# A hybrid decoder trunk: transposes moved out of gate and up, and 64-byte offsets for the last moving weights and the cross queries

## The chip, the cores and the metric

The kernel runs on one core of a Trainium2 chip. The metric is the device time of one execution in microseconds (us). Times of before are the median of three timed runs; one more execution was recorded by the hardware profiler, and every row shown comes from it.

## The reference

Two layers of a decoder trunk work on x of 256 tokens x 1024 features, in float32. Each layer adds four blocks to x, each on an RMS-normalised copy:

```python
for l in range(DEPTH):                       # DEPTH = 2, SEQ = 256, D_MODEL = 1024, D_FF = 2816
    x = x + 0.5 * swiglu(rms_norm(x, ffn1_norm[l]), ffn1_w_gate[l], ffn1_w_up[l], ffn1_w_down[l])
    x = x + hybrid_mixer(rms_norm(x, mix_norm[l]), w_in[l], ...)       # HGRN2 heads | FoX heads
    x = x + memory_cross_attention(rms_norm(x, cross_norm[l]), rms_norm(mem, mem_norm[l]), ...)
    x = x + 0.5 * swiglu(rms_norm(x, ffn2_norm[l]), ffn2_w_gate[l], ffn2_w_up[l], ffn2_w_down[l])
return rms_norm(x, final_norm)

def swiglu(h, w_gate, w_up, w_down):
    return (jax.nn.silu(h @ w_gate) * (h @ w_up)) @ w_down
```

The cross attention has 4 heads of 256 features against 256 memory tokens. All weights together are some 217 MB, read once.

## The kernel before

**Products.** Each float32 operand is split into a high part, its cast to fp32r, and a low part, the rest. A product is then three matmuls that add up in PSUM: high by high, high by low, low by high. `mm3` (L448) issues them from lines 449, 450 and 451. In the names of a matmul, `out<-a,b` lists the moving operand `a` first and the stationary one `b` second: the array holds `b` (128 x 128), a LDWEIGHTS loads it, and `a` streams through with 256 or 512 columns. TensorE loads the next `b` while it streams the present `a`.

**Two forms of a projection.** `xstat` and `xstat_first` keep the features `xf` stationary and stream 512 weight columns (`acc<-whi,xfh`, 128x512); the result has tokens on the partitions. `wstat` (L573) keeps weights stationary and streams the 256 tokens (`acc<-xfh,whi`, 128x256); the result has features on the partitions. A feed-forward (`ffn`, L686) takes its 2816 hidden features in six chunks (`FCH`): chunk 0 by `xstat_first`, the other five by `wstat`, gate and then up. Since chunk 0's product `sil` has tokens on the partitions, the task `h_task` (L691) turns it with eight transposes `hp` (L700), and ACT and DVE write its split `hth`, `htl`. In the first feed-forward `first_chunk` does chunk 0 on x itself and turns the factors of the norm with two transposes `rt` (L565). `rows_to_residual` (L644) then does the down projection: for each 128 hidden features, 12 matmuls of 512 columns.

**Weights.** `plan` lists all weight pieces in the order of use. SP issues their loads into three `raw` buffers; ACT casts the high part `whi`, DVE subtracts to get the low part `wlo` (`split`, L177), into seven slots of `wp`. Each entry of `plan` has a `lead`: the place in the slot, in elements of 4 bytes, where the piece begins. It is `LEAD` = 16 (64 bytes) for weights that become stationary and 0 for those that stream. The slots and the buffers of pool `sp` (tag `s4`, which hold `xf`, `hth`, `kc` and `qc` among others) are whole multiples of 256 bytes long and begin at the same place modulo 256. So `lead` alone sets how the address of a weight lies to that of a feature, modulo 256 bytes: 0 or 64.

**Order.** The program is written by `drive` (L410), which runs generators as tasks on an estimated clock; `yield (LAT_HT,)` puts a task's next step that much later, and an `Event` lets it wait for another task. Each engine then does its instructions in the order in which they were written. `lower_bounds` (L312) is one such task: it waits 20 us and 6 us, turns a small table by the transpose `lbt` (L317) and works out the gates' bounds on ACT and DVE. In `cross` (L1115), `head` computes one head's scores `cs` from keys `kc` (moving) and queries `qc` (stationary), and its softmax `pp` is turned and split into `ppT`.

Of the kernel before, what the change touches and what calls it, by code (L numbers as in the profile page):

```python
# [17 lines left out]
P = 128  # L18
# [7 lines left out]
EPS = 1e-6  # L26
NEG = -1.0e30
FCH = [(c, min(512, DFF - c)) for c in range(0, DFF, 512)]

ROWS, LEAD = 1024, 16  # L30
SLOT = ROWS + 128
APART = 64
N_S4, N_W = 19, 7
TAIL = 6
HP = 100
LA_D, LA_S = 3, 1
# [1 line left out]
LAT_LVL, LAT_AX, LAT_HN = 4.0, 1.5, 5.2  # L38
LAT_FS, LAT_FT, LAT_CQ, LAT_CS, LAT_CT = 7.0, 3.5, 2.6, 5.6, 3.0
LAT_Q, LAT_G1, LAT_G2, LAT_M = 5.0, 9.0, 2.0, 18.0  # L40
LAT_HT = 2.4
LAT_FK, LAT_LANE = 6.5, 2.8

OFF_Q, OFF_F, OFF_I, OFF_G = 0, 512, 1024, 1536
# [4 lines left out]
def hymba_kernel(  # L49
# [9 lines left out]
    rawp = ctx.enter_context(tc.tile_pool(name="rawp", bufs=3))  # L59
    wp = ctx.enter_context(tc.tile_pool(name="wp", bufs=N_W))  # L60
    sp = ctx.enter_context(tc.tile_pool(name="sp", bufs=N_S4))
    np_ = ctx.enter_context(tc.tile_pool(name="np", bufs=1))
    sm = ctx.enter_context(tc.tile_pool(name="sm", bufs=4))
    psa = ctx.enter_context(tc.tile_pool(name="psa", bufs=4, space=PSUM))
# [17 lines left out]
    def smp(name="smp"):  # L82
        return pss.tile([P, 512], F32, name=nm(name), tag="smp")

    sp.tile([P, APART], F32, name="apart", tag="apart", bufs=1)
    xs = cp.tile([P, NT, D], F32, name="xs")


# [2 lines left out]
    def kview(w, l, c0, cw, k0, nk):  # L91
        return w[l, k0 * P:(k0 + nk) * P, c0:c0 + cw].rearrange("(k p) c -> p k c", p=P)

    def add_cols(w, l, c0, cw, scaled=None, lead=LEAD):
        for k0 in range(0, KT, 4):
            plan.append((kview(w, l, c0, cw, k0, 4), 4, cw, (scaled[0], scaled[1] + k0) if scaled else None, lead))

    def add_rows(w, l, nkt):
        for k0 in range(0, nkt, 2):
            plan.append((kview(w, l, 0, D, k0, 2), 2, D, None, 0))  # L100

    def add_ffn(g, u, d, l, scaled=None):
        for c0, cw in FCH:
            for w in (g, u):
                add_cols(w, l, c0, cw, scaled, LEAD if c0 else 0)
        add_rows(d, l, FT)

    for l in range(DEPTH):
        add_ffn(ffn1_g, ffn1_u, ffn1_d, l, ("first", 0) if l == 0 else None)
        for o in (OFF_I, OFF_G, OFF_F, OFF_Q):  # L110
            add_cols(w_in, l, o, 512, None, 0 if o in (OFF_I, OFF_G) else LEAD)
        add_cols(w_in, l, OFF_FV + 260, 260, None, 0)
        add_cols(w_in, l, OFF_FQ, 512)
        add_cols(w_in, l, OFF_FK, 512)
        add_cols(w_in, l, OFF_FV, 260, None, 0)
        of_mem = ("mem", 8 * l)
        add_cols(c_wk, l, 0, 512, of_mem)
        add_cols(c_wk, l, 512, 512, of_mem)
        add_cols(c_wv, l, 0, 512, of_mem, 0)
        add_rows(w_out, l, KT)  # L120
        add_cols(c_wv, l, 512, 512, of_mem, 0)
        for c0 in (0, 512):
            add_cols(c_wq, l, c0, 512)
        add_rows(c_wo, l, KT)
        add_ffn(ffn2_g, ffn2_u, ffn2_d, l)

    raws = []
# [73 lines left out]
    def take():  # L201
        i = taken[0]
        taken[0] += 1
        split(i + LA_S)
        return pieces[i]
# [106 lines left out]
    def lower_bounds():  # L312
        nc.sync.dma_start(out=lbr[0:8], in_=hgrn_lb.rearrange("d (h p) -> (d h) p", p=P))
        nc.sync.dma_start(out=lbr[8:24], in_=mem_norm.rearrange("d (k p) -> (d k) p", p=P))
        yield (6.0,)
        pt = smp("lbt")
        nc.tensor.transpose(pt[:, 0:24], lbr, ident[0:24, 0:24])  # L317
# [10 lines left out]
        nc.scalar.activation(e, e, AF.Exp)  # L328
# [74 lines left out]

    clock = [0.0]
    tasks = []

    def spawn(gen):
        tasks.append([gen, clock[0], None])
# [45 lines left out]
        mm3(ps[t][:, :cw], f.hi(kt, t), f.lo(kt, t), pc[0], pc[1], kt == 0, kt == KT - 1)  # L454
        return 3 * 0.107 * max(1.0, cw / 256.0)

    def xstat(f, cw, ps):
        ps += [acc() for _ in range(NT)]
        for kb in range(2):
            pc = take()  # L460
            for j in range(4):
                c = 0.0
                for t in range(NT):
                    c += xmm(ps, f, 4 * kb + j, t, pc[j], cw)
                yield c
# [23 lines left out]
    def first_chunk(f, psa_, psb_):  # L489
# [67 lines left out]
            for t in range(NT):  # L557
                inv_rms(sums[t], rs[t])
        yield 16 * T512
        yield from xstat(f, 512, psb_)  # L560
        rb = sq[0].rearrange("p (j t) -> p j t", j=8)
        pt = smp("rt")
        for t in range(NT):
            nc.vector.tensor_scalar(out=rb[:, t, :], in0=ident, scalar1=0.0, scalar2=rs[t], op0=ALU.mult, op1=ALU.add)
            nc.tensor.transpose(pt[:, t * P:(t + 1) * P], rb[:, t, :], ident)  # L565
        row = sm.tile([P, S], F32, name=nm("L"), tag="L", bufs=1)
        nc.vector.tensor_copy(out=row, in_=pt[:, 0:S])
# [118 lines left out]
    def ffn(cur, nxt_w, last=False, first=False):  # L686
        f = cur.f
        hts = {}
        evs = [Event() for _ in FCH]

        def h_task(c, hs, cw):  # L691
            yield (LAT_HT,)
            nk = cw // P
            hi = s4([P, 4, S], F32R, "hth")
            lo = s4([P, 4, S], F32R, "htl")
            hts[c] = (hi, lo)
            for t in range(NT):
                pt = smp("hp")
                for j in range(nk):
                    nc.tensor.transpose(pt[:, j * P:(j + 1) * P], hs[:, t, j * P:(j + 1) * P], ident)  # L700
# [18 lines left out]
        for ci, (c0, cw) in enumerate(FCH):  # L719
# [7 lines left out]
            else:  # L727
# [20 lines left out]

                yield from wstat(f, use_u, cw)
                evs[ci].fire(3.0)  # L750
        nxt = Next(nxt_w, last)

        def act(kt, t):
            hi, lo = hts[kt // 4]
            return hi[:, kt % 4, t * P:(t + 1) * P], lo[:, kt % 4, t * P:(t + 1) * P]

        yield from rows_to_residual(act, FT, scale, TAIL, nxt, lambda kt: evs[kt // 4])
        return nxt


    def hgrn(q, f, k, v, gw, oT, masks, ready, done):
# [96 lines left out]
            yield 4 * T1  # L858
        done.fire(1.6)


    def pp(rows=P, dt=F32):
        return sm.tile([rows, 512], dt, name=nm("pp"), tag="pp", bufs=4)

    def fox_gates(zb, L_, R_, tri, sel, done):

# [63 lines left out]
    def fox_lane(lane, fq, fk, fv, L_, R_, oT, cmask, oh, ready, done):  # L930
        yield ready
        for pr in (lane, lane + 2):
# [22 lines left out]
            for sub in range(2):  # L955
                pt = smp("fpt")
                for j in range(3):
                    nc.tensor.transpose(pt[:, j * P:(j + 1) * P], prs[sub][:, j * P:(j + 1) * P], ident)
                yield 3 * T1
                pT = sm.tile([P, 512], F32, name=nm("ppT"), tag="ppT", bufs=4)  # L960
# [154 lines left out]
    def cross(cur, kc, vc, mf, nxt_w):  # L1115
# [4 lines left out]
        def head(c, b, qh, ql):  # L1120
# [21 lines left out]
            ph = sm.tile([P, 512], F32R, name=nm("ppT"), tag="ppT", bufs=4)  # L1142
            pl = sm.tile([P, 512], F32R, name=nm("ppT"), tag="ppT", bufs=4)
            put_split(ph, pl, pt)
            yield (LAT_CT,)
            po = smp("cpo")
# [14 lines left out]
        for c in range(2):  # L1161
            oT.alloc(c)

            def use(b, psq):
                q2 = s4([P, 2, 2, S], F32R, "qc")
                put_split(q2[:, 0], q2[:, 1], psq.rearrange("p (k t) -> p k t", k=2))
                spawn(head(c, b, q2[:, 0], q2[:, 1]))

            yield from wstat(f, use)
        nxt = Next(nxt_w)  # L1170
# [8 lines left out]
    def trunk():  # L1179
# [2 lines left out]

        def early():
            yield (20.0,)
            yield from lower_bounds()
            consts.extend(consts_mixer())

        spawn(early())
        for l in range(DEPTH):
# [34 lines left out]
```

## Time and profile before

| what | value |
|---|---|
| median of three timed runs | 1221.28 us (1220.73 to 1222.85) |
| the profiled execution | 1216.61 us, of it 1214.8 us from its first to its last instruction |
| busy: PE, weight loads (PEld), DVE, ACT | 1201.1, 1104.8, 769.8, 651.5 us |
| matmuls of lines 449 to 451 | 2534 of each line |
| read from HBM | 216.23 MB, 179 GB/s over the span |

A matmul's own duration is longer than the step to the next one, since matmuls overlap in the array: with 256 columns it reads about 0.28 us, with 512 about 0.39 us. The step between the starts of two neighbours tells the pace. "Idle before" is time in which an engine had nothing to do ahead of an instruction, and the releaser behind the arrow is what ended it. Because PE is nearly always busy, the rows to look at are those of PE's pace, not of waits.

### The profile page before, as it was taken

The page shows a single profiled execution, that of the slowest core. Times are in us where ns is not written, and L with a number is a line of the kernel's source. Part 1 is how long each engine was busy: PE and PEld are TensorE (multiplying, and loading weights), DVE is VectorE, ACT ScalarE, POOL GpSimd, SP SyncE. Part 2 cuts the span into 40 slices and gives each one's busy share as a digit, 9 for nine tenths or more (in the row PEclk, how much of TensorE's full clock was granted, in tenths as well). Part 3 has the DMA queues.
Part 4 walks back from the last instruction along what each step waited for, and adds up shares of the span by engine and source line. Part 5 has one row for each costly group of instructions (what it writes and reads, how often), then busy time and mean ns, then how long its engine had stood idle before and what let it go on. Part 6 is the DMA issues. An engine that isn't in the chain of part 4 may idle for free.

```text
span 1214.8 us, 21577 instructions
## 1 busy us (share of the span) xinstructions
PE 1201.1 (99%) x9037; PEld 1104.8 (91%) x9037; DVE 769.8 (63%) x1194; ACT 651.5 (54%) x1022; POOL 37.7 (3%) x50
## 2 busy tenths in 40 slices
PE   9999999999999999999999999999999999999997
PEld 7999888999889889998889998889988898999986
DVE  6966647488866675464474565476787766655643
ACT  7665535578854454354264454266686555544532
POOL 0000000011000000000000000000110000000000
PEclk9999999999999999999999999999999999999999
DMA  8655655544544374566474556464444534555740
GB/s 300 209 193 184 246 174 191 176 141 139 197 142 165 106 259 150 198 204 213 139 252 147 208 188 229 139 226 158 144 154 171 193 119 139 183 201 174 245 172 35
DMA packets 100002, 218.68 MB, mean 180 GB/s; under 512 B 4128, under 2 KB 16704, under 8 KB 99904
## 3 DMA queue, kind: packets, MB, share of 16 engines
q1 hardware_dynamic: 99744, 217.03, 52.6%
q8 instruction: 71, 1.16, 0.4%
q10 hardware_dynamic: 160, 0.27, 0.1%
q14 instruction: 27, 0.22, 0.1%
HBM read 216.23 MB, written 1.05 MB: 179 GB/s over the span
## 4 chain that ended last, share of the span: by engine, by line
PE 87%; DVE 5%; ACT 4%; issue 2%; POOL 1%; DMA 1%; POOLq 0%; SPq 0%; ACTq 0%
PE acc L449 27%; PE acc L451 27%; PE acc L450 27%; DVE wlo L154 1%; ACT whi L157 1%; DVE wlo L158 1%; PE acc L512 1%; DMA mem<-in_mem_dram 1%; PE pt L370 1%; POOL rs L351 1%; PE al L778 0%; ACT whi L153 0%; DVE xfl L377 0%; ACT pp L902 0%; POOL hrs L847 0%
## 5 line engine op out<-in xcount | busy, mean ns | idle before, releaser
L154 DVE TENSOR_TENSOR wlo<-raw,whi 128x1024 fp32r<-128x1024 f32 (+1 forms) x332 | 389.6, 1196 | 255.3 <-ACT whi L153 253.0
L153 ACT CAST whi<-raw 128x1024 fp32r<-128x1024 f32 (+1 forms) x332 | 331.9, 1029 | 263.9 <-PE acc L451 126.7
L449 PE MATMUL acc<-xfh,whi 128*128 128x256 f32 x1536 | 428.8, 279 | 0.0
L451 PE MATMUL acc<-xfh,wlo 128*128 128x256 f32 x1536 | 427.1, 278 | 0.9 <-DVE wlo L154 0.9
L450 PE MATMUL acc<-xfl,whi 128*128 128x256 f32 x1536 | 427.1, 278 | 0.8 <-DVE xfl L377 0.8
L449 PEld LDWEIGHTS acc<-xfh,whi 128*128 128x128 f32 x1536 | 290.0, 189 | 0.8
L450 PEld LDWEIGHTS acc<-xfl,whi 128*128 128x128 f32 x1536 | 289.2, 188 | 1.4 <-DVE xfl L377 1.3
L451 PEld LDWEIGHTS acc<-xfh,wlo 128*128 128x128 f32 x1536 | 288.4, 188 | 1.3 <-DVE wlo L154 1.3
L449 PE MATMUL acc<-whi,hth 128*128 128x512 f32 (+1 forms) x352 | 135.0, 384 | 0.0
L450 PE MATMUL acc<-wlo,hth 128*128 128x512 f32 (+1 forms) x352 | 134.8, 383 | 0.0
L451 PE MATMUL acc<-whi,htl 128*128 128x512 f32 (+1 forms) x352 | 134.6, 383 | 0.0
L449 PE MATMUL acc<-whi,xfh 128*128 128x512 f32 (+1 forms) x240 | 87.3, 364 | 0.0
L451 PE MATMUL acc<-whi,xfl 128*128 128x512 f32 (+1 forms) x240 | 86.6, 361 | 0.0
L450 PE MATMUL acc<-wlo,xfh 128*128 128x512 f32 (+1 forms) x240 | 86.5, 360 | 0.0
L451 PEld LDWEIGHTS acc<-whi,htl 128*128 128x128 f32 x352 | 66.1, 188 | 13.0
L449 PEld LDWEIGHTS acc<-whi,hth 128*128 128x128 f32 x352 | 66.2, 188 | 12.9
L450 PEld LDWEIGHTS acc<-wlo,hth 128*128 128x128 f32 x352 | 66.2, 188 | 12.8
L158 DVE SCALAR_TENSOR_TENSOR wlo<-raw,g,whi 128x512 fp32r<-128x512 f32 (+1 forms) x96 | 62.0, 702 | 18.7 <-ACT whi L157 18.7
L157 ACT ACTIVATE whi<-raw,g 128x512 fp32r<-128x512 f32 (+1 forms) x96 | 58.3, 677 | 17.4 <-PE acc L450 13.7
L376 ACT CAST hth<-sil 128x512 fp32r<-128x512 f32 x36 | 22.3, 620 | 55.4 <-DVE sil L745 55.4
L451 PEld LDWEIGHTS acc<-whi,xfl 128*128 128x128 f32 x240 | 45.1, 188 | 6.9
L449 PEld LDWEIGHTS acc<-whi,xfh 128*128 128x128 f32 x240 | 45.1, 188 | 6.9
(274 smaller groups left out, 1543.2 us busy)
## 6 DMA issues: line engine op xcount, KB each, us to landing
raw<-in_ffn_w_down_dram SPq DMA_DIRECT2D x44, 1024.0 KB, 4.9
raw<-in_ffn_w_up_dram SPq DMA_DIRECT2D x40, 1024.0 KB, 5.3
raw<-in_ffn_w_gate_dram SPq DMA_DIRECT2D x38, 1024.0 KB, 5.2
raw<-in_w_in_dram SPq DMA_DIRECT2D x24, 1024.0 KB, 5.2
raw<-in_cross_wk_dram SPq DMA_DIRECT2D x8, 1024.0 KB, 5.1
raw<-in_cross_wv_dram SPq DMA_DIRECT2D x8, 1024.0 KB, 5.4
raw<-in_w_out_dram SPq DMA_DIRECT2D x8, 1024.0 KB, 4.9
raw<-in_cross_wq_dram SPq DMA_DIRECT2D x8, 1024.0 KB, 5.1
```

Of the source, the lines that this page charges most:

```text
L153: nc.scalar.copy(out=hi, in_=sl)
L154: nc.vector.tensor_tensor(out=lo, in0=sl, in1=hi.bitcast(F32), op=ALU.subtract)
L157: nc.scalar.mul(hi, sl, g)
L158: nc.vector.scalar_tensor_tensor(out=lo, in0=sl, scalar=g, in1=hi.bitcast(F32), op0=ALU.mult, op1=ALU.subtract)
L351: nc.gpsimd.tensor_tensor(out=rs, in0=ms, in1=neghalf[:, 0:1], op=ALU.pow)
L370: nc.tensor.transpose(pt[:, j * P:(j + 1) * P], hn[:, kt * P:(kt + 1) * P], ident)
L376: nc.scalar.copy(out=hi, in_=src)
L449: nc.tensor.matmul(ps, lhsT=lh, rhs=rh, start=start, stop=False)
L450: nc.tensor.matmul(ps, lhsT=lh, rhs=rl, start=False, stop=False)
L451: nc.tensor.matmul(ps, lhsT=ll, rhs=rh, start=False, stop=stop)
L512: nc.tensor.matmul(psa_[t], lhsT=x, rhs=w, start=kt == 0 and which == 0, stop=kt == KT - 1 and which == 1)
```

## The change

Three things change, with what they need.

1. *Gate and up without transposes.* `h_task` waits for the event `all_up`, fired when the last up projection has been written, in place of 2.4 us. The down projection takes k-tiles 4 to 11 first, then chunk 0's 0 to 3, then the rest (`DOWN`), and its weights are planned in that order. `lower_bounds` waits for the same point of the first feed-forward (`up_done`) in place of 6 us (and `consts_mixer`, which follows it, is written ahead of it), and `rt` moves between the two halves of the first up projection.
2. *Lead by piece.* `lead` becomes a pair, one for each half (4 k-tiles) of a column block: `STAT` (16, 16), `MOVE` (0, 0), `LAST` (0, 16). `LAST` stands at the three places where streamed weights come right ahead of stationary ones: the up projection of chunk 0, the mixer's `OFF_G`, and the second half of the cross values.
3. *Cross queries.* `qc` leaves pool `sp`; its high and low parts become two `pp` tiles, in a new pool `ap` with six of them, behind a filler of 320 bytes. `ppT` moves to the same pool. The scratch for dynamic DMAs shrinks from 8192 to 4096 bytes.

```diff
+DOWN = [*range(4, 12), *range(4), *range(12, FT)]
-N_S4, N_W = 19, 7
+N_S4, N_W, N_PP = 19, 7, 6
-LAT_HT = 2.4
+    ap = ctx.enter_context(tc.tile_pool(name="ap", bufs=1))
+    ap.tile([P, 80], F32, name="apart_pp", tag="apart_pp")
...
-    def add_cols(w, l, c0, cw, scaled=None, lead=LEAD):
+    STAT, MOVE, LAST = (LEAD, LEAD), (0, 0), (0, LEAD)
+
+    def add_cols(w, l, c0, cw, scaled=None, lead=STAT):
         for k0 in range(0, KT, 4):
-            plan.append((kview(w, l, c0, cw, k0, 4), 4, cw, (scaled[0], scaled[1] + k0) if scaled else None, lead))
+            plan.append((kview(w, l, c0, cw, k0, 4), 4, cw, (scaled[0], scaled[1] + k0) if scaled else None,
+                         lead[k0 // 4]))
...
         for c0, cw in FCH:
-            for w in (g, u):
-                add_cols(w, l, c0, cw, scaled, LEAD if c0 else 0)
-        add_rows(d, l, FT)
+            add_cols(g, l, c0, cw, scaled, STAT if c0 else MOVE)
+            add_cols(u, l, c0, cw, scaled, STAT if c0 else LAST)
+        add_rows(d, l, DOWN)
...
-        for o in (OFF_I, OFF_G, OFF_F, OFF_Q):
-            add_cols(w_in, l, o, 512, None, 0 if o in (OFF_I, OFF_G) else LEAD)
+        for o, lead in ((OFF_I, MOVE), (OFF_G, LAST), (OFF_F, STAT), (OFF_Q, STAT)):
+            add_cols(w_in, l, o, 512, None, lead)
...
-        add_cols(c_wv, l, 512, 512, of_mem, 0)
+        add_cols(c_wv, l, 512, 512, of_mem, LAST)
...
     def lower_bounds():
...
-        yield (6.0,)
+        yield up_done
         pt = smp("lbt")
...
-    def xstat(f, cw, ps):
+    def xstat(f, cw, ps, between=None):
         ps += [acc() for _ in range(NT)]
         for kb in range(2):
+            if kb and between is not None:
+                between()
...
-        yield from xstat(f, 512, psb_)
-        rb = sq[0].rearrange("p (j t) -> p j t", j=8)
...
+        def turn_rs():
+            rb = sq[0].rearrange("p (j t) -> p j t", j=8)
...
+        yield from xstat(f, 512, psb_, turn_rs)
...
+        all_up = Event()
         def h_task(c, hs, cw):
-            yield (LAT_HT,)
+            yield all_up
...
                 yield from wstat(f, use_u, cw)
                 evs[ci].fire(3.0)
+        all_up.fire()
+        if first:
+            up_done.fire()
         nxt = Next(nxt_w, last)
-        def act(kt, t):
+        def act(i, t):
+            kt = DOWN[i]
             hi, lo = hts[kt // 4]
...
-                q2 = s4([P, 2, 2, S], F32R, "qc")
-                put_split(q2[:, 0], q2[:, 1], psq.rearrange("p (k t) -> p k t", k=2))
-                spawn(head(c, b, q2[:, 0], q2[:, 1]))
+                qh, ql = (pp(P, F32R).rearrange("p (k t) -> p k t", k=2) for _ in range(2))
+                put_split(qh, ql, psq.rearrange("p (k t) -> p k t", k=2))
+                spawn(head(c, b, qh, ql))
```

In the second feed-forward of layer 0, TensorE's order before has the eight transposes 27 matmuls into the 256-column stream (`xf` are the features, `whi` and `wlo` weights):

```order
L449 MATMUL acc_5067<-xfh_4805,whi_5009 128x256
L450 MATMUL acc_5067<-xfl_4806,whi_5009 128x256
L451 MATMUL acc_5067<-xfh_4805,wlo_5010 128x256
L700 MATMUL hp_5097<-ident,sil_5041 128x128 x4
L700 MATMUL hp_5104<-ident,sil_5041 128x128 x4
L449 MATMUL acc_5067<-xfh_4805,whi_5009 128x256
L450 MATMUL acc_5067<-xfl_4806,whi_5009 128x256
L451 MATMUL acc_5067<-xfh_4805,wlo_5010 128x256
```

In the same feed-forward after the change, they stand between the last up matmul and the first of the down projection (`hth`, `htl` are the split hidden features):

```order
L455 MATMUL acc_6120<-xfh_4816,whi_6106 128x256
L456 MATMUL acc_6120<-xfl_4817,whi_6106 128x256
L457 MATMUL acc_6120<-xfh_4816,wlo_6107 128x256
L713 MATMUL hp_6190<-ident,sil_5050 128x128 x4
L713 MATMUL hp_6197<-ident,sil_5050 128x128 x4
L455 MATMUL acc_6174<-whi_6112,hth_5176 128x512
L456 MATMUL acc_6174<-wlo_6113,hth_5176 128x512
```

All 864 matmuls of 256 columns of a feed-forward now follow each other. In the first feed-forward, before, TensorE's two transposes `rt` stand between the last 512-column matmul and the first of 256 columns:

```order
L449 MATMUL acc_256<-whi_279,xfh_125 128x512
L450 MATMUL acc_256<-wlo_280,xfh_125 128x512
L451 MATMUL acc_256<-whi_279,xfl_126 128x512
L565 MATMUL rt_347<-ident,sq_131 128x128 x2
L449 MATMUL acc_392<-xfh_123,whi_311 128x256
L450 MATMUL acc_392<-xfl_124,whi_311 128x256
```

After the change they stand 24 matmuls earlier, between the halves of the up projection, and the two kinds of matmul meet directly:

```order
L455 MATMUL acc_261<-whi_284,xfh_129 128x512
L456 MATMUL acc_261<-wlo_285,xfh_129 128x512
L457 MATMUL acc_261<-whi_284,xfl_130 128x512
L455 MATMUL acc_396<-xfh_127,whi_322 128x256
L456 MATMUL acc_396<-xfl_128,whi_322 128x256
```

The rows of TensorE, ACT and DVE at all other places keep their order, and SP issues the same loads in the same order but for the rows of the down weights.

More of the change, by code (lines that the diff above doesn't have):

```diff
@@ L92, in kview, with add_rows @@
         return w[l, k0 * P:(k0 + nk) * P, c0:c0 + cw].rearrange("(k p) c -> p k c", p=P)
-    def add_cols(w, l, c0, cw, scaled=None, lead=LEAD):
+    STAT, MOVE, LAST = (LEAD, LEAD), (0, 0), (0, LEAD)
+    def add_cols(w, l, c0, cw, scaled=None, lead=STAT):
         for k0 in range(0, KT, 4):
-            plan.append((kview(w, l, c0, cw, k0, 4), 4, cw, (scaled[0], scaled[1] + k0) if scaled else None, lead))
-    def add_rows(w, l, nkt):
-        for k0 in range(0, nkt, 2):
+            plan.append((kview(w, l, c0, cw, k0, 4), 4, cw, (scaled[0], scaled[1] + k0) if scaled else None,
+                         lead[k0 // 4]))
+    def add_rows(w, l, rows):
+        for k0 in rows[::2]:
             plan.append((kview(w, l, 0, D, k0, 2), 2, D, None, 0))
@@ L103, in add_ffn @@
         for c0, cw in FCH:
-            for w in (g, u):
-                add_cols(w, l, c0, cw, scaled, LEAD if c0 else 0)
-        add_rows(d, l, FT)
+            add_cols(g, l, c0, cw, scaled, STAT if c0 else MOVE)
+            add_cols(u, l, c0, cw, scaled, STAT if c0 else LAST)
+        add_rows(d, l, DOWN)
     for l in range(DEPTH):
         add_ffn(ffn1_g, ffn1_u, ffn1_d, l, ("first", 0) if l == 0 else None)
-        for o in (OFF_I, OFF_G, OFF_F, OFF_Q):
-            add_cols(w_in, l, o, 512, None, 0 if o in (OFF_I, OFF_G) else LEAD)
-        add_cols(w_in, l, OFF_FV + 260, 260, None, 0)
+        for o, lead in ((OFF_I, MOVE), (OFF_G, LAST), (OFF_F, STAT), (OFF_Q, STAT)):
+            add_cols(w_in, l, o, 512, None, lead)
+        add_cols(w_in, l, OFF_FV + 260, 260, None, MOVE)
         add_cols(w_in, l, OFF_FQ, 512)
         add_cols(w_in, l, OFF_FK, 512)
-        add_cols(w_in, l, OFF_FV, 260, None, 0)
+        add_cols(w_in, l, OFF_FV, 260, None, MOVE)
         of_mem = ("mem", 8 * l)
@@ L118, in hymba_kernel @@
         add_cols(c_wk, l, 512, 512, of_mem)
-        add_cols(c_wv, l, 0, 512, of_mem, 0)
-        add_rows(w_out, l, KT)
-        add_cols(c_wv, l, 512, 512, of_mem, 0)
+        add_cols(c_wv, l, 0, 512, of_mem, MOVE)
+        add_rows(w_out, l, range(KT))
+        add_cols(c_wv, l, 512, 512, of_mem, LAST)
         for c0 in (0, 512):
             add_cols(c_wq, l, c0, 512)
-        add_rows(c_wo, l, KT)
+        add_rows(c_wo, l, range(KT))
         add_ffn(ffn2_g, ffn2_u, ffn2_d, l)
@@ L405, in hymba_kernel @@
     tasks = []
+    up_done = Event()
     def spawn(gen):
@@ L559, in first_chunk @@
         yield 16 * T512
-        yield from xstat(f, 512, psb_)
-        rb = sq[0].rearrange("p (j t) -> p j t", j=8)
[L562 to L565, printed above, removed]
-        row = sm.tile([P, S], F32, name=nm("L"), tag="L", bufs=1)
-        nc.vector.tensor_copy(out=row, in_=pt[:, 0:S])
+        row = sm.tile([P, S], F32, name=nm("L"), tag="L", bufs=1)
+        def turn_rs():
+            rb = sq[0].rearrange("p (j t) -> p j t", j=8)
+            pt = smp("rt")
+            for t in range(NT):
+                nc.vector.tensor_scalar(out=rb[:, t, :], in0=ident, scalar1=0.0, scalar2=rs[t], op0=ALU.mult,
+                                        op1=ALU.add)
+                nc.tensor.transpose(pt[:, t * P:(t + 1) * P], rb[:, t, :], ident)
+            nc.vector.tensor_copy(out=row, in_=pt[:, 0:S])
+        yield from xstat(f, 512, psb_, turn_rs)
         hrs = [small(1, "hrs0", bufs=2) for _ in range(NT)]
@@ L750, in ffn @@
                 evs[ci].fire(3.0)
+        all_up.fire()
+        if first:
+            up_done.fire()
         nxt = Next(nxt_w, last)
-        def act(kt, t):
+        def act(i, t):
+            kt = DOWN[i]
             hi, lo = hts[kt // 4]
             return hi[:, kt % 4, t * P:(t + 1) * P], lo[:, kt % 4, t * P:(t + 1) * P]
-        yield from rows_to_residual(act, FT, scale, TAIL, nxt, lambda kt: evs[kt // 4])
+        yield from rows_to_residual(act, FT, scale, TAIL, nxt, lambda i: evs[DOWN[i] // 4])
         return nxt
@@ L859, in hgrn, with ppt @@
         done.fire(1.6)
+    apart_ppt = []
     def pp(rows=P, dt=F32):
-        return sm.tile([rows, 512], dt, name=nm("pp"), tag="pp", bufs=4)
+        return ap.tile([rows, 512], dt, name=nm("pp"), tag="pp", bufs=N_PP)
+    def ppt(dt=F32):
+        if not apart_ppt:
+            apart_ppt.append(ap.tile([P, 96], F32, name="apart_ppT", tag="apart_ppT"))
+        return ap.tile([P, 512], dt, name=nm("ppT"), tag="ppT", bufs=4)
     def fox_gates(zb, L_, R_, tri, sel, done):
@@ L959, in fox_lane @@
                 yield 3 * T1
-                pT = sm.tile([P, 512], F32, name=nm("ppT"), tag="ppT", bufs=4)
+                pT = ppt()
                 nc.scalar.copy(out=pT[:, 0:3 * P], in_=pt[:, 0:3 * P])
@@ L1141, in head @@
             yield 4 * T1
-            ph = sm.tile([P, 512], F32R, name=nm("ppT"), tag="ppT", bufs=4)
-            pl = sm.tile([P, 512], F32R, name=nm("ppT"), tag="ppT", bufs=4)
+            ph, pl = ppt(F32R), ppt(F32R)
             put_split(ph, pl, pt)
@@ L1184, in early @@
             yield (20.0,)
+            consts.extend(consts_mixer())
             yield from lower_bounds()
-            consts.extend(consts_mixer())
         spawn(early())
@@ L1209 @@
     from concourse.bass_utils import run_bass_kernel_spmd as _run
-    nc = _bacc.Bacc("TRN2", target_bir_lowering=False, num_devices=1, dynamic_dma_scratch_size=8192)
+    nc = _bacc.Bacc("TRN2", target_bir_lowering=False, num_devices=1, dynamic_dma_scratch_size=4096)
     arrays, args = {}, []
```

## The prediction

> **What bounds the kernel now.** I read the page first, then TensorE's waits, then the same stage of four places side by side, then single instructions where a stage begins. The page's busy rows come first.
>
> ```profile
> span 1214.8 us, 21577 instructions
> ...
> PE 1201.1 (99%) x9037; PEld 1104.8 (91%) x9037; DVE 769.8 (63%) x1194; ACT 651.5 (54%) x1022; POOL 37.7 (3%) x50
> ...
> PE 87%; DVE 5%; ACT 4%; issue 2%; POOL 1%; DMA 1%; POOLq 0%; SPq 0%; ACTq 0%
> ```
>
> TensorE has work in 99% of the span and is 87% of the chain that ended last. The waits of PE say how little of it is waiting:
>
> ```profile
> PE warm L234 <- POOL ident masks.py:199: 1.4, 1, 1.4
> PE acc L451 <- DVE wlo L154: 0.9, 2, 0.5
> PE acc L450 <- DVE xfl L377: 0.8, 2, 0.4
> ```
>
> No wait is over 1.4 us. So only TensorE's own pace can give more than 1 us. Five windows of that pace follow (PE's busy time, the count of matmuls that touch the window, clock, DMA share, GB/s). The first four lie in the gate/up stages of feed-forward 2 of layer 0, 1 of layer 1, 1 of layer 0, 2 of layer 1; the fifth is the mixer's f and q projection. All are the same 256-column matmul.
>
> ```profile
> 455.00:545.00 90.00, 90.00 (x766) 1.00 0.53 178
> 643.00:733.00 90.00, 90.00 (x796) 1.00 0.58 196
> 52.00:128.00 76.00, 76.00 (x673) 1.00 0.59 191
> 1057.00:1145.00 88.00, 88.00 (x779) 1.00 0.56 192
> 215.00:236.00 21.00, 21.00 (x181) 1.00 0.53 175
> ```
>
> A matmul lasts 0.28 us and overlaps the next ones, so the step from one to the next is (window + 0.28) / count: 117.9 ns in the first row, 113.4, 113.3 and 113.3 in the next three, 117.6 in the last. There are two paces, 4.5 ns apart, at full clock and with no wait, and each holds for a whole stage. The grouped rows show the same: slow stage first, fast stage second, each with its matmul and its weight load.
>
> ```profile
> L449 PE MATMUL acc<-xfh,whi 128*128 128x256 f32 x199 | 55.9, 281 | 0.0
> L449 PEld LDWEIGHTS acc<-xfh,whi 128*128 128x128 f32 x199 | 38.2, 192 | 0.0
> ...
> L449 PE MATMUL acc<-xfh,whi 128*128 128x256 f32 x207 | 57.1, 276 | 0.0
> L449 PEld LDWEIGHTS acc<-xfh,whi 128*128 128x128 f32 x206 | 38.7, 188 | 0.0
> ```
>
> A slow matmul reads 281 ns and a fast one 276; the weight load of L449 takes 192 instead of 188. I read this as two reads of SBUF that get in each other's way: TensorE streams one operand while it loads the next weights, and in the slow pace they meet.
>
> **Where the pace is set.** The 256-column stream of feed-forward 2, layer 0 begins right behind 512-column matmuls; 27 matmuls later the eight transposes `hp` break in:
>
> ```profile
> 447.93 0.39 PE L451 MATMUL acc<-whi,xfl 128*128 128x512 f32 x1
> 448.16 0.28 PE L449 MATMUL acc<-xfh,whi 128*128 128x256 f32 x1
> 448.28 0.28 PE L450 MATMUL acc<-xfl,whi 128*128 128x256 f32 x1
> ...
> 451.22 0.28 PE L451 MATMUL acc<-xfh,wlo 128*128 128x256 f32 x1
> 451.35 1.03 PE L700 MATMUL hp<-ident,sil 128*128 128x128 f32 x8
> 452.13 0.36 PE L449 MATMUL acc<-xfh,whi 128*128 128x256 f32 x1
> ```
>
> From 448.16 to 451.22 there are 26 steps, 117.7 ns each: the stream is slow from its first matmul, and the first window above shows it slow behind the transposes as well. In layer 1 the same place goes another way:
>
> ```profile
> 634.22 0.28 PE L449 MATMUL acc<-xfh,whi 128*128 128x256 f32 x1
> ...
> 637.28 0.28 PE L451 MATMUL acc<-xfh,wlo 128*128 128x256 f32 x1
> 637.40 1.04 PE L700 MATMUL hp<-ident,sil 128*128 128x128 f32 x8
> 638.19 0.37 PE L449 MATMUL acc<-xfh,whi 128*128 128x256 f32 x1
> ...
> 638.63 0.28 PE L449 MATMUL acc<-xfh,whi 128*128 128x256 f32 x1
> ...
> 639.99 0.28 PE L449 MATMUL acc<-xfh,whi 128*128 128x256 f32 x1
> ```
>
> It enters slow (26 steps in 3.06 us, 117.7 ns) and leaves the transposes fast (12 steps in 1.36 us, 113.3 ns). In feed-forward 1 of layer 0 the single transpose `lbt` makes the turn:
>
> ```profile
> 48.36 0.28 PE L451 MATMUL acc<-xfh,wlo 128*128 128x256 f32 x1
> 48.57 0.24 PE L317 MATMUL lbt<-ident,lbr 24*128 24x24 f32 x1
> 48.74 0.39 PE L449 MATMUL acc<-xfh,whi 128*128 128x256 f32 x1
> 48.96 0.28 PE L450 MATMUL acc<-xfl,whi 128*128 128x256 f32 x1
> ```
>
> So every stream that follows 512-column matmuls without a gap starts slow here, and a break by transposes sometimes frees it. The change takes all breaks away from gate and up and alters the addresses of the last 512-column operands.
>
> **The change, part by part.** The baseline of the sum is the profiled execution, 1216.61 us (its span 1214.8). The median of the runs shown is 1221.28, 4.67 above it. That is about one gate/up stage in the other pace (837 x 4.5 ns = 3.8 us), so I expect the timed executions to have one stage more in the slow pace; this is an estimate.
>
> *The offset of the last moving weights.* With it, the transition into each 256-column stream pairs a moving operand and a weight load at the same offset (modulo 256 bytes), where it was 64 bytes; and the half piece before it goes from 0 to 64 the other way. No row shows either pairing at such a place. The nearest rows say that the relation of the two addresses does set the pace, so I take it that the entry becomes fast; the two ends are all entries fast and all entries slow as now. If fast:
> - feed-forward 2 of layer 0: gate and up after the first 512 columns are 2 x 18 column tiles x 8 k-tiles x 3 = 864 matmuls, all slow now: 864 x 4.5 = 3.9 us.
> - feed-forward 1 of layer 0: the 27 + 114 matmuls ahead of `lbt` are slow: 141 x 4.5 = 0.6 us.
> - the first 27 of the other two stages: 54 x 4.5 = 0.2 us.
> - the mixer's f and q in both layers: 2 x 192 x 4.5 = 1.7 us.
>
> The 512-column matmuls at the new offset are 24 in each of 8 places, 192. Their step now is 226.8 ns ((30 + 0.39) / 134):
>
> ```profile
> 140.00:170.00 30.00, 30.00 (x134) 24.86 (x133) 13.48 (x11) 11.72 (x12) 0.00 (x0) 1.00 0.53 182
> ```
>
> Weight loads fill only 24.86 of 30 us there, so a late load has room. I take 0, with 0 and 192 x 9 ns = 1.7 us as ends (9 is twice the 4.5 of the shorter matmul).
>
> *The transposes.* Eight `hp` per feed-forward move from the 256-column stream to its end, ahead of the first down matmul; none is removed. Now they take 451.35 to 452.13, 0.78 us, and then too: 0. Their casts and subtractions (2 + 2 instructions) then stand beside the down projection, whose weight casts and splits leave gaps:
>
> ```profile
> 139.25 1.05 ACT L153 CAST whi<-raw 128x1024 fp32r<-128x1024 f32 x1 [1.68 <-PE acc L451]
> ...
> 140.33 1.22 DVE L154 TENSOR_TENSOR wlo<-raw,whi 128x1024 fp32r<-128x1024 f32 x1 [1.50 <-ACT whi L153]
> ```
>
> ACT idles 1.68 us and DVE 1.50 us ahead of each, and the result is wanted only at the ninth k-tile, 8 x 12 x 0.227 = 21.8 us later. The two `rt` move ahead of 24 matmuls of 512 columns, from 30.78 to 30.78 - 24 x 0.227 = 25.3 us; their input is there by 23.8:
>
> ```profile
> 30.78 0.38 PE L565 MATMUL rt<-ident,sq 128*128 128x128 f32 x2
> ...
> 23.33 0.48 DVE L564 TENSOR_SCALAR sq<-ident,rs 128x128 f32<-128x128 f32 x2
> ```
>
> So 1.5 us of cover remain; without it PE would wait for what is missing. `lbt` moves next to `hp`: the rows above show 48.36 to 48.96, 0.60 us, for two steps of 0.12 and one small transpose, so about 0.25 us of drain that I take as saved (ends 0 and 0.36). Its chain on ACT and DVE, moves from the gate/up stage to the start of down, with a table load:
>
> ```profile
> 50.76 1.28 ACT L328 ACT_TABLE_LOAD   x1
> ```
>
> Behind it on ACT stand weight casts, and DVE's splits behind those; 1.28 us fits into the 1.68 us of idle time: 0 (without that cover, the 1.28). No DMA is issued elsewhere in the queue; only the order of the rows of W_down changes.
>
> *Cross queries.* The scores' 96 matmuls step at 120 ns (9 steps in 1.08 us):
>
> ```profile
> 375.89 0.28 PE L449 MATMUL cs<-kc,qc 128*128 128x256 f32 x1
> ...
> 376.97 0.28 PE L449 MATMUL cs<-kc,qc 128*128 128x256 f32 x1
> ```
>
> Here both operands lie in one pool, at offset 0; then they lie 64 bytes apart, as in the two paces above. That gives 96 x (2.2 to 6.7) = 0.2 to 0.6 us; I take 0.3. The query projections between them are slow in part now (up to 168 matmuls, 0.75 us); they begin behind a wait that the offset can't reach, so 0.2.
>
> Sum: 3.9 + 0.6 + 0.2 + 1.7 + 0.25 + 0.3 + 0.2 = 7.1 us, 1209.5 against the profiled execution. If the 4.67 us are a stage in the slow pace, they go as well; if they are something else they stay (1214.2). I take the nearer end and a third of the way: 1211.
>
> The Trainium skill, SBUF — State Buffer, section "Who interferes with whom", says that TensorE's two read ports, one for the moving operand and one for weight loads, are independent and that PE never waits on anyone. By it no address could change a matmul's step, the offsets would be worth 0, and the time would be that of the first rival. The 120 ns row and the 192 ns weight load speak against it; this transition no row shows.
>
> **The rivals.**
> - *The offset does nothing, every stream stays in the pace of its entry.* For it: the gapless entries at 448.16 and 634.22, and the f and q window, are slow. Against: the pace of pairs at offset 0 differs (120 ns). Then the 723 matmuls behind `lbt` and 2 x 837 behind `hp`, fast today, turn slow: 2397 x 4.5 = 10.8 us more, less 0.55 for `lbt` and the scores: 1226.9, slower by 0.5%. The median of before is reached when three of the four gate/up stages are slow from their entry (3 x 3.9 = 11.7 us over the sum).
> - *The pace at entry falls by chance, stage by stage.* For it: the same transposes freed layer 1 and not layer 0. Four stages of 3.9 and two of 0.85 us, half of them slow, put it at 1209.5 + 8.6 = 1218, in steps of 3.9.
> - *A new wait takes it back:* a faster feed-forward 2 needs weights sooner. Against it: the fast stage at 643 to 733 runs with DMA at 0.58 and its grouped rows show no idle time. It would eat that stage's 3.9 us: 1213.4.
>
> **How the numbers follow.** No change is within 0.2%, 2.4 us, about what a measurement of this kernel can tell. Forecast (all entries fast) 0.55; no effect 0.20, of which 0.17 slower and 0.03 same; chance 0.20, split 0.10, 0.05 and 0.05 between faster, same and slower; a new wait 0.05 (0.03, 0.01, 0.01). So faster 0.68, same 0.09, slower 0.23. Range: the forecast alone holds 1207 to 1215; the chance case reaches 1222, and the no-effect case lies at 1226.9 or, if the 4.67 us stay, at 1231.6. So 1206 to 1227 leaves out the upper half of the last (0.10) and little else.
>
> **What would show it.** In the profile after: right if the first matmul behind the 512-column ones steps at 113 ns and the grouped rows of all four gate/up stages and of f and q read 276 ns and 188 ns; the scores 276 to 281 instead of 283. Wrong if those rows read 281 or 283 in the stages that are fast today, or if PE waits for `rt` near 25 us or for weights in feed-forward 2. A time near 1227 with 281 everywhere would mean that the transposes, not the addresses, were what made stages fast.

## Result and profile after

The changed kernel takes 1211.49 us (median of 12 runs, 1209.69 to 1216.35), the one before 1220.78 us in the same comparison (12 runs, 1216.51 to 1223.48). The ratio is 0.9933, with a 95% interval of 0.9916 to 0.995: faster by 0.7%. The profiled execution takes 1209.70 us (its span 1207.9), against 1216.61 (1214.8) before: 6.91 us less. That execution of before is one of its faster ones, so the two profiles lie closer together than the medians, which are 9.29 us apart. The page's first lines, and the chain of waits:

```profile
span 1207.9 us, 21582 instructions
...
PE 1194.0 (99%) x9037; PEld 1097.0 (91%) x9037; DVE 769.1 (64%) x1194; ACT 651.5 (54%) x1022; POOL 37.7 (3%) x50
...
PE 86%; DVE 5%; ACT 4%; issue 2%; POOL 1%; DMA 1%; POOLq 0%; SPq 0%; ACTq 0%; DVEq 0%
```

TensorE does as many matmuls as before, is busy for 7.1 us less, and is still busy for 99% of the span. So its pace has changed, not its waits, of which the longest in the view of PE's waits are these (all others take 0.7 us or less in total, but one of 1.1 for `fs` in the mixer):

```profile
PE warm L239 <- POOL ident masks.py:199: 1.4, 1, 1.4
PE acc L457 <- DVE wlo L159: 1.2, 2, 0.7
```

None of PE's waits lies in feed-forward 2, so a new wait there, the prediction's third rival, did not come.

The windows of that pace, in the order of before (feed-forward 2 of layer 0, 1 of layer 1, 1 of layer 0, 2 of layer 1, the mixer's f and q):

```profile
450.00:540.00 90.00, 90.00 (x796) 1.00 0.55 184
635.00:725.00 90.00, 90.00 (x796) 1.00 0.55 188
50.00:126.00 76.00, 76.00 (x673) 1.00 0.60 196
1045.00:1133.00 88.00, 88.00 (x779) 1.00 0.53 183
215.00:235.00 20.00, 20.00 (x178) 1.00 0.54 184
```

(window + 0.28) / count is 113.4, 113.4, 113.3, 113.3 and 113.9 ns. The first and the last were 117.9 and 117.6 before. The grouped rows of feed-forward 2, layer 0, from 500.0 to 524.1 us, now read 276 and 188 ns, where they read 281 and 192:

```profile
L455 PE MATMUL acc<-xfh,whi 128*128 128x256 f32 x72 | 19.9, 276 | 0.0
...
L455 PEld LDWEIGHTS acc<-xfh,whi 128*128 128x128 f32 x71 | 13.3, 188 | 0.0
```

The timeline of PE where that stage begins and ends:

```profile
446.49 0.40 PE L457 MATMUL acc<-whi,xfl 128*128 128x512 f32 x1
446.73 0.28 PE L455 MATMUL acc<-xfh,whi 128*128 128x256 f32 x1
446.84 0.28 PE L456 MATMUL acc<-xfl,whi 128*128 128x256 f32 x1
...
544.67 1.04 PE L713 MATMUL hp<-ident,sil 128*128 128x128 f32 x8
545.46 0.48 PE L455 MATMUL acc<-whi,hth 128*128 128x512 f32 x1
```

From 446.73 to 544.67 there are 864 steps, 113.4 ns each: the stream starts in the fast pace and keeps it to its last matmul. The sums of the steps from one start to the next, over all matmuls of each kind, give the whole account:

| part | us before | us after | difference | predicted |
|---|---|---|---|---|
| gate/up, feed-forward 2, layer 0 | 101.86 | 97.94 | -3.92 | -3.9 |
| gate/up, feed-forward 1, layer 0 | 98.94 | 98.03 | -0.91 | -0.6 and -0.25 (`lbt`) |
| gate/up, the other two stages | 196.28 | 195.88 | -0.40 | -0.2 |
| mixer f and q, both layers | 45.22 | 43.56 | -1.66 | -1.7 |
| cross queries, both layers | 45.24 | 43.91 | -1.33 | -0.2 |
| scores `cs` | 11.66 | 11.19 | -0.47 | -0.3 |
| 512-column matmuls of `xf` | 133.45 | 134.00 | +0.55 | 0 |
| other 256-column matmuls of the mixer | 48.65 | 49.20 | +0.54 | not in the sum |
| everything else | | | +0.69 | not in the sum |

### The profile page after: what moved, and what is told of

Read it like the earlier page. It is cut to its first block, busy times and chain, and to the rows that moved or that the text cites. A ratio compares the mean times of both kernels' runs of the same rounds, so it can differ in the third digit from the quotient of the medians.

```text
span 1207.9 us, 21582 instructions
## 1 busy us (share of the span) xinstructions
PE 1194.0 (99%) x9037; PEld 1097.0 (91%) x9037; DVE 769.1 (64%) x1194; ACT 651.5 (54%) x1022; POOL 37.7 (3%) x50
## 4 chain that ended last, share of the span: by engine, by line
PE 86%; DVE 5%; ACT 4%; issue 2%; POOL 1%; DMA 1%; POOLq 0%; SPq 0%; ACTq 0%; DVEq 0%
PE acc L455 27%; PE acc L456 26%; PE acc L457 26%; DVE wlo L159 1%; ACT whi L162 1%; DVE wlo L163 1%; PE acc L520 1%; DMA mem<-in_mem_dram 1%; PE pt L375 1%; POOL rs L356 1%; ACT whi L158 1%; PE al L795 0%; DVE xfl L382 0%; ACT pp L926 0%; PE cpo L456 0%
```

## The experiments

The theory: the addresses of the operands at the entry set the pace of a 256-column stream, and the stream keeps that pace until something breaks in. The rivals: the transposes alone made the stages fast; or the pace falls by chance.

**The transposes out, without the offset.**

```diff
-    STAT, MOVE, LAST = (LEAD, LEAD), (0, 0), (0, LEAD)
+    STAT, MOVE, LAST = (LEAD, LEAD), (0, 0), (0, 0)
```

> The changed kernel with the last moving weights back at offset 0 (LAST = (0, 0)); transposes stay out of gate and up. Theory (the address pair at the entry sets the pace of the whole stream): all four gate/up streams and both f,q streams enter slow and stay slow: 4 x 864 x 4.4 ns + 2 x 192 x 4.4 ns = 16.9 us more, less 0.55 us for the 512-column matmuls: 1209.7 + 16.3 = 1226 us, with rows of 281 and 192 ns. Rival 1 (taking the transposes out is what made the stages fast): no stage changes, 1209 to 1211 us. Rival 2 (the pace at the entry falls by chance): some stages slow, some fast, near 1218 us.

Measured: 1226.47 us (1226.26 to 1227.21, 5 runs), ratio 1.0049 (1.0032 to 1.0066). Windows of feed-forward 2 and 1 and of f and q, and grouped rows of one stage:

```profile
451.00:550.00 99.00, 99.00 (x843) 1.00 0.54 183
637.00:735.00 98.00, 98.00 (x835) 1.00 0.53 184
...
218.00:240.00 22.00, 22.00 (x189) 1.00 0.49 171
...
L455 PE MATMUL acc<-xfh,whi 128*128 128x256 f32 x69 | 19.4, 281 | 0.0
...
L456 PEld LDWEIGHTS acc<-xfl,whi 128*128 128x128 f32 x68 | 13.1, 192 | 0.0
```

117.8, 117.7 and 117.9 ns: each stream is slow from its first matmul to its last. The first rival falls: without the offset, taking the transposes out costs 5.7 us. The second falls for gapless entries in these profiles: all six streams went the same way, and the five times lie within 1 us, where one gate/up stream is worth 3.9.

**The offset without the rest.** The kernel before, with `lead` as a pair and `LAST` at the same three places:

```diff
-            for w in (g, u):
-                add_cols(w, l, c0, cw, scaled, LEAD if c0 else 0)
+            add_cols(g, l, c0, cw, scaled, STAT if c0 else MOVE)
+            add_cols(u, l, c0, cw, scaled, STAT if c0 else LAST)
```

> The kernel before with the lead by piece alone (LAST at the same three places); all transposes stay inside gate and up, and qc stays where it was. Theory: all entries are fast (first 27 steps of feed-forward 1 of layer 1 and of both feed-forwards 2 at 113 ns, f,q at 113 ns). If a break by transposes keeps the pace of the stream, feed-forward 2 of layer 0 is fast as well: 1216.6 - 3.9 - 0.6 - 0.2 - 1.7 + 0.5 = 1210.7 us; if a break draws the pace anew, each stage can fall back for 3.7 us, and only 2.0 us are sure: up to 1214.6, or more if other stages fall back. Rival (taking the transposes out did it): entries slow, f,q at 117.6 ns, 1216 to 1221 us as before.

Measured: 1224.74 us (1222.41 to 1227.01, 10 runs), ratio 1.0033 (1.0019 to 1.0046). This lies above every number named: 1214.6 "or more if other stages fall back", and the rival's 1221. All four gate/up stages fell back. The timeline of feed-forward 2, layer 0, then windows behind its `hp`, behind that of feed-forward 1, layer 1, and of f and q:

```profile
450.95 0.28 PE L452 MATMUL acc<-xfh,whi 128*128 128x256 f32 x1
...
454.03 1.04 PE L703 MATMUL hp<-ident,sil 128*128 128x128 f32 x8
454.83 0.36 PE L452 MATMUL acc<-xfh,whi 128*128 128x256 f32 x1
...
456.00:550.00 94.00, 94.00 (x801) 1.00 0.52 180
642.00:735.00 93.00, 93.00 (x792) 1.00 0.53 179
...
218.00:239.00 21.00, 21.00 (x187) 1.00 0.52 178
```

The entry is fast (27 steps in 3.08 us, 114.1 ns), the stream behind the transposes slow (117.7 and 117.8 ns); f and q, which nothing breaks, are fast (113.8 ns). Feed-forward 1 of layer 0 shows the turn at the single transpose `lbt` as well; windows ahead of it and behind it:

```profile
36.00:48.00 12.00, 12.00 (x108) 1.00 0.53 173
49.00:130.00 81.00, 81.00 (x690) 1.00 0.57 194
```

113.7 ns ahead, 117.8 behind. (There the stream still comes in behind `rt`, at 118 ns, and `hp` sets it free.) In this profile a break turned a fast stream slow four times out of four (three `hp`, one `lbt`). In the profile of before, where all streams came in slow, a break made them fast in three cases out of five. So the two parts work only together: the offset alone costs 4.0 us, the removal alone (with the moved queries) 5.7, both gain 9.3, each against the median of before in its own comparison.

**Which part of the last block matters.** First the lead on the other half, then twice the lead, then the lead on the last of the eight k-tiles alone:

```diff
-LAST = (LEAD, LEAD), (0, 0), (0, LEAD)
+LAST = (LEAD, LEAD), (0, 0), (LEAD, 0)          # run 1
+LAST = (LEAD, LEAD), (0, 0), (0, 2 * LEAD)      # run 2
+# run 3: LAST = (0, None); None: the last k-tile begins at step + LEAD, the others at 0
+at, gap = (0, step + (LEAD if k0 else 0)) if lead is None else (lead, step)
```

> The changed kernel with the lead on the first half of the last moving block instead of the second (LAST = (16, 0)): 24 matmuls of 512 columns still run with the load at -64, but the 24 behind them are at offset 0 and the pair at the entry is at 64 bytes again. Theory (the last pair, or the last few, sets the pace of the entry): all entries slow as with LAST = (0, 0), 1226 to 1227 us. Rival (the disturbed 512-column steps shift the phase, and the shift lasts): entries fast, 1210 to 1215 us.

> The changed kernel with LAST = (0, 32): the last half of the moving block begins 128 bytes off, so that the pair at the entry is at -64 (192) instead of 0, and the 24 matmuls ahead of it at 128. Theory (only a pair at offset 0 enters fast): slow, 1226 to 1228 us. Rival (any offset but 64 enters fast): 1210 to 1215 us, with the 512-column steps of that half at 229 to 234 ns.

> The changed kernel with the lead on the last k-tile of the last moving block alone: 6 matmuls of 512 columns in each place run with the load at -64 instead of 24, and the pair at the entry is at offset 0 as in the changed kernel. Theory (the last pair sets the entry): fast entries, and the 0.55 us that the 512-column matmuls lost shrink to about 0.15: 1209 to 1214 us, not to be told from the changed kernel but by its rows. Rival (the shift of the whole half is needed): entries slow, 1226 us.

Measured: 1228.12 us (ratio 1.0085, 1.0058 to 1.0112), 1227.07 us (1.0077, 1.0051 to 1.0103) and 1211.13 us (0.994, 0.9922 to 0.9958). One window of feed-forward 2, layer 0, of each:

```profile
451.00:550.00 99.00, 99.00 (x843) 1.00 0.53 183
```

```profile
455.00:553.00 98.00, 98.00 (x835) 1.00 0.54 184
```

```profile
447.00:544.00 97.00, 97.00 (x858) 1.00 0.56 194
```

117.8, 117.7 and 113.4 ns, and so in the other stages. The disturbed 512-column steps do not carry over; the last six matmuls decide. A stream whose own weights lie 64 bytes off the features comes in fast when the last moving operand and the first weight load have the same offset modulo 256 bytes; with 64 or 192 bytes between them it comes in slow. The third run also saves what it was expected to save. In feed-forward 2 of layer 0, the last 24 matmuls of 512 columns step at 226.7 ns without the offset, at 229.6 in the changed kernel and at 227.9 here. Over all eight places these stretches take 0.40 us more in the changed kernel than without the offset, and 0.13 more here. The sum over all 512-column matmuls of `xf` (133.86 us here, 134.00 in the changed kernel) hides it, since it varies on its own: it is 134.49 in the second profile of the changed kernel, below. The time can't be told from that of the changed kernel.

**Other distances in the stream itself.** `LEAD` = 32, 48, 8 and 24 in place of 16 move the stationary weights to 128, 192, 32 and 96 bytes from the features; the pair at the entry stays at 0.

```diff
-ROWS, LEAD = 1024, 16
+ROWS, LEAD = 1024, 32      # then 48, 8, 24
```

> The changed kernel with LEAD = 32 instead of 16: stationary weights lie 128 bytes off the features, and the pair at the entry stays at offset 0. Theory (the relation of the two addresses sets the step): the 256-column step takes another value or has other paces than 113.3 and 117.8 ns; no row shows 128 bytes. Between no interference worth the name (109 ns, the step of the transposes hp: 4608 x 4.4 = 20 us less, 1190 us) and that of offset 0 (120 ns: 4608 x 6.6 = 30 us more, 1240 us); I lean to the fast pace, 1205 to 1212 us. Rival (only same or not the same offset matters): 1210 to 1214 us as the changed kernel.

> The changed kernel with LEAD = 48: stationary weights lie 192 bytes (that is -64) off the features; the 512-column matmuls of the last piece have the load 64 bytes ahead of the moving operand instead of behind. Theory (the relation with its sign sets the step): the 256-column step differs from that at +64; the scores of after at +64 step 113 and the 512-column ones at -64 lost 2.5 ns, so I expect a slower step here, 115 to 120 ns, 1217 to 1240 us. Rival (only same or not the same offset matters): 113.4 ns, 1210 to 1214 us.

> The changed kernel with LEAD = 8: stationary weights 32 bytes off the features, the entry at offset 0. The runs so far show 120 ns at 0 and 128 bytes, and the two paces 113.3 and 117.8 at 64 and 192. Theory (what counts is the 64-byte block, even or odd): 32 bytes lie in the same block as 0, 120 ns, 1209.7 + 4608 x 6.5 ns = 1239 us at most, 1235 to 1240. Rival (the distance in bytes counts, so that 32 lies between): 113 to 118 ns, 1205 to 1230 us.

> The changed kernel with LEAD = 24: stationary weights 96 bytes off the features, the entry at offset 0. Theory (64-byte blocks, even or odd): 96 bytes is in the block of 64, so the paces are 113.3 or 117.8 ns, with fast entries as at 64: 1210 to 1215 us. Rival (the distance in bytes counts, 96 lies between 64 and 128): 115 to 120 ns, 1218 to 1240 us.

Measured: 1236.87 us (ratio 1.0134, 1.0108 to 1.0159), 1229.04 (1.0069, 1.0047 to 1.0091), 1232.38 (1.0096, 1.0081 to 1.0111) and 1231.99 (1.0093, 1.0079 to 1.0107). The window of feed-forward 2, layer 0, in each, in that order; of the last also feed-forward 1, layer 0:

```profile
454.00:550.00 96.00, 96.00 (x802) 1.00 0.51 176
```

```profile
452.00:550.00 98.00, 98.00 (x834) 1.00 0.53 183
```

```profile
454.00:550.00 96.00, 96.00 (x814) 1.00 0.53 181
```

```profile
453.00:550.00 97.00, 97.00 (x820) 1.00 0.53 181
32.00:130.00 98.00, 98.00 (x838) 1.00 0.62 202
```

The steps are 120.0 ns at 128 bytes (118.7 in feed-forward 1 of layer 0), 117.8 at 192, 118.3 at 32, and 118.6 and 117.3 at 96. Streams at 192 bytes reach 113.3 ns too, in cross and between the mixer's small matmuls (48 query matmuls in 5.44 us), so 64 and 192 share the two paces; but at 192 an entry at 0 leads to the slow one. My reading by even and odd 64-byte blocks held for 0, 64, 128 and 192 and failed for 32 and 96: those lie between, as the rival had it. The lean to "1205 to 1212" for 128 bytes was a miss. Of the six distances seen (0 bytes in the scores alone), 64 bytes with a fast entry is the best.

**The cross queries back at offset 0.**

```diff
-    ap.tile([P, 80], F32, name="apart_pp", tag="apart_pp")
+    ap.tile([P, 64], F32, name="apart_pp", tag="apart_pp")
```

> The changed kernel with the filler ahead of pp 64 bytes shorter, so that qc lies at offset 0 to kc again (the filler ahead of ppT is 64 bytes longer, and ppT stays). Theory: the 96 score matmuls step at 120 ns again, 96 x 5 = 0.5 us more, and the query projections between them may fall to 118 (up to 2 x 0.5 us); gate, up, f and q stay fast: 1210 to 1215 us with the rows of cs at 283 ns. Rival (where qc lies matters for more, since it took room from the pool of the features): over 1216 us.

Measured: 1211.88 us (1210.31 to 1213.27), ratio 0.9953 (0.9937 to 0.997). The scores by tile (minimum, median and maximum duration), in the changed kernel, then in this one:

```profile
L456 PE MATMUL cs<-kc,pp x32: 276/276/281, 375.0 to 995.1; 128*128 128x256 f32 x32
```

```profile
L456 PE MATMUL cs<-kc,pp x32: 279/283/283, 376.0 to 997.0; 128*128 128x256 f32 x32
```

The 96 scores sum to 11.66 us, as before the change, against 11.19: 0.47 us. The query matmuls sum to 44.3 us against 43.9. That alone says little, for they sum to 44.6 in the second profile of the changed kernel, below. The 48 query matmuls behind the first scores say more. With `qc` at 0 they step at 117.8 ns in both layers (here, before the change, and in the run of the offset alone), though in five of these six places the query matmuls ahead of the scores are fast. With `qc` at 64 bytes they keep the pace of those ahead: 113.3 ns in both layers of the changed kernel, and in its second profile 113.3 in layer 0 and 117.8 in layer 1, where the ones ahead were slow too. Two stretches of 48 at 4.5 ns are 0.4 us. So the move of `qc` is worth up to 0.9 us, below what the times can tell; gate, up, f and q stayed fast.

**A candidate, and the changed kernel once more.** The candidate is run 3 above with the 260-column weights at `STAT`:

```diff
-        add_cols(w_in, l, OFF_FV + 260, 260, None, MOVE)
+        add_cols(w_in, l, OFF_FV + 260, 260, None, STAT)
```

(and the same for `OFF_FV`).

> A candidate: the lead on the last k-tile alone, and the 260-column weights of the mixer (FV) at STAT instead of MOVE, so that their matmuls run with the load at -64 instead of at offset 0. Now these 192 matmuls have a median step of 119 ns. Theory (odd 64-byte offsets step at 113.3 or 117.8 with 256 columns): 192 x (1 to 5 ns) = 0.2 to 1.0 us less, 1208.5 to 1213 us; not to be told from the changed kernel by the times. Rival (streaming weights with the load behind, as the 512-column ones: a few ns more): 0.2 to 0.6 us more.

> The changed kernel once more, nothing altered, beside the candidate on the same chip. Theory: all four gate/up streams and f,q enter fast again, in this profile as in the first, and the times lie at 1209.7 to 1216 us. Rival (the entry still falls by chance): at least one stream shows 281 ns and 192 ns, 3.9 us more for a gate/up stream.

Measured on the same chip: candidate 1210.26 us (1209.7 to 1210.74), ratio 0.9914 (0.99 to 0.9927); changed kernel 1210.41 us (1209.82 to 1214.12), 0.9921 (0.9908 to 0.9933). That is no difference. The grouped row of the 260-column matmuls, changed kernel and then candidate:

```profile
L456 PE MATMUL acc<-wlo,xfh 128*128 128x260 f32 x64 | 18.0, 281 | 0.0
```

```profile
L457 PE MATMUL acc<-wlo,xfh 128*128 128x260 f32 x64 | 18.0, 282 | 0.0
```

Their steps sum to 23.73 us against 23.53: the rival was right, 0.2 us are lost. The second profile of the changed kernel has all four gate/up streams and f and q fast again. These are two of its windows, feed-forward 2 of layer 0 (113.4 ns) and of layer 1 (113.3 ns):

```profile
447.00:544.00 97.00, 97.00 (x858) 1.00 0.56 190
...
1043.00:1139.00 96.00, 96.00 (x850) 1.00 0.56 191
```

One of its five executions, 1214.12 us, lies 3.8 us above the mean of the others, about the price of one gate/up stream. It was not profiled, so a slow entry in it is not ruled out.

## Why the prediction was right, and where it was not

- **The entry.** Right, in sign and in size: 3.92 us for feed-forward 2 of layer 0 and 1.66 for f and q, where 3.9 and 1.7 stood. It rested on a guess from far rows (that the pair at the entry counts, and that equal offsets there are the good case). Equal offsets *inside* a stream give the slowest step seen, 120 ns (as 128 bytes do); at the entry into a stream at 64 bytes they are the best.
- **The size of the rival.** "No effect, all slow" was priced at 1226.9; the kernel without the offset takes 1226.47.
- **The transposes.** Their work was rightly costed at nothing: `hp` takes 0.79 us at its new place (544.67 to 545.46), and PE waits nowhere for `rt` (no wait of PE names it). What the prediction did not say is that a break turns a *fast* stream slow. It read breaks as something that frees a stream, and so had no price for the offset alone: the sum's terms look separate and are not.
- **`lbt`.** Predicted 0.25 us saved. The timeline now:

```profile
128.92 0.28 PE L457 MATMUL acc<-xfh,wlo 128*128 128x256 f32 x1
129.13 0.24 PE L322 MATMUL lbt<-ident,lbr 24*128 24x24 f32 x1
129.30 1.09 PE L713 MATMUL hp<-ident,sil 128*128 128x128 f32 x8
```

  It still takes 0.38 us from the last matmul to `hp`, 0.27 above a step, where it took 0.36 before: 0.1 saved.
- **The 512-column matmuls.** Taken as 0, since a late load "has room". Their sum grew by 0.55 us, of which the offset made 0.40 (the last 24 at the eight places), inside the stated ends of 0 and 1.7. Room in the load's busy time does not show that nothing is delayed.
- **The cross queries.** Mis-sized, 0.2 against 1.33 us. The count was short: of the 384 query matmuls 302 read 279 to 283 ns before, not up to 168, and 29 do in the first profile after. The view that a wait shields them was wrong in part: the offset reaches the 48 behind the first scores, for about 0.4 us. The rest varies from one profile to the next: in the second profile of the changed kernel one stretch of 78 query matmuls runs at 118 ns that ran at 113 in the first, and all queries take 0.7 us more.
- **The baseline.** The profiled execution was forecast at 1209.5 and came out at 1209.70, because +0.55, +0.54 and +0.69 us, none of them in the sum, met gains 1.5 us larger than forecast, 1.3 of them in cross. That it came so close is luck. The third of 4.67 us then met the median, 1211 against 1211.49, by luck rather than by reasoning. Runs of before lie in two groups, near 1216.7 and near 1221, some 4 us apart, the price of one stage. That fits breaks that turn out differently from one execution to the next; no profile of the upper group was taken, so it isn't shown.

The Trainium skill's SBUF — State Buffer, section "Who interferes with whom", gives TensorE two independent read ports and says that it never waits on anyone. These runs differ from it: with nothing changed but where the weights begin, the same matmul steps at 113.4, 117.8, 118.3 or 120.0 ns. Why the reads disturb each other is not shown; only the address relation was varied.

## What to carry to other kernels

Where an engine is busy all the time, compare its step in places that do the same work: a difference of 4% with no wait is a second pace, and here addresses and breaks set it. Such a pace can outlive what caused it, so look at the entry of a long stream and at what interrupts it, and try parts of a change together as well as alone: here each part alone made the kernel slower. Costs that are below what the times can tell can still be read from the rows of one operation.

## What the hardware showed unexpectedly

The memory of the pace was the surprise: six 512-column matmuls decide how the next 864 matmuls run, 98 us long. Another part of the scatter sits at the start. In the profile of the run with twice the lead (1230.21 us, the slowest of its five), the 512-column matmuls of the first chunk step at 0.43 us until 13.3 us and at 0.23 us from then on, while the granted clock reads 1.00:

```profile
10.74 0.63 PE L520 MATMUL acc<-whi,xfh 128*128 128x512 f32 x1
11.17 0.63 PE L520 MATMUL acc<-whi,xfl 128*128 128x512 f32 x1
...
13.66 0.40 PE L520 MATMUL acc<-whi,xfl 128*128 128x512 f32 x1
13.90 0.39 PE L520 MATMUL acc<-whi,xfh 128*128 128x512 f32 x1
...
6.00:13.00 7.00, 6.73 (x18) 1.00 1.02 378
```

Its first 256-column stream begins at 33.78 us, that of the changed kernel at 31.10. The Trainium skill, TensorE: Matmul & The Clock Gate, section "What's actually happening", tells of a clock at half rate until TensorE has been busy for a while; a step near twice the later one agrees with that. So 2.7 us of scatter can come from the start alone. Six of the changed kernel's 12 executions lie 2.7 to 6.7 us above its fastest, and their cause is not shown: none of its executions above 1210.59 us was profiled. A gate/up stream in the slow pace would cost 3.9 us, so it is not shown that all streams enter fast in every execution.
